# A decoder step on one core: second feed-forward weights in the other half's input buffers, closer decode gathers, spaced late loads

## The chip, the core and the metric

The kernel runs on one of the eight cores of a Trainium2 chip. A core has TensorE (PE, matrix products, with PEld its weight load), VectorE (DVE), ScalarE (ACT), GpSimd (POOL) and SyncE (SP, which here only issues transfers). Each engine executes its own instructions in order; semaphores order them against each other. The metric is the device time of one execution in microseconds (us), as the median of several runs.

## What is computed

One step of one hybrid decoder layer, for a prompt of 1024 tokens and for 8 samples with one new token each, whose past of 8192 tokens lies in a paged cache. All data are float32. The reference, cut to what matters:

```python
h = modulate(x, sh1, sc1)                        # layer norm, then shift and scale from c
sb_q, sb_k, sb_v, g_q, g_k, g_v, g_r, g_low, br_a, br_b = split(h @ w_in)
o_sb = sb_attend(sb_q, concat(past_k, sb_k), concat(past_v, sb_v), sb_bias)   # stick-breaking attention
o_g  = gla_mix(g_q, g_k, g_v, log_a, S0)         # gated linear attention, then norm and gate
merged = sigmoid(br_a) * (o_sb @ w_up_a) + sigmoid(br_b) * (o_g @ w_up_b)
x1 = layer_norm(ALPHA * x + gt1 * (merged @ w_o))
h2 = modulate(x1, sh2, sc2)
f  = square(relu(h2 @ w_ff1)) @ w_ff2            # 1024 -> 4096 -> 1024
x2 = layer_norm(ALPHA * x1 + gt2 * f)
```

It runs for the prompt (without a past) and for the samples (with the pages of the past, 268 MB of keys and values).

## The kernel before

**Precision.** A matmul of the prompt is made of three in the type float32r: each operand is split by `split` into a high part (`h`, copied by ACT) and a low part (`l`, the difference, by POOL or DVE), and high x high, low x high and high x low are added up in PSUM (`three`). So each weight tile is loaded raw by SP (`load_split`), split by ACT and POOL, and only then used by PE.

**Emission by an account.** The program is written out in one order by `Flow`: generators for the main stream (`main`), for two other streams and for many small tasks yield times or conditions; `Engines` keeps an account of when each engine and each tile would be ready, and the next piece of work is emitted where the account says it fits. `until(tiles)` waits for tiles to be ready by the account, `calm(t)` waits until DVE's backlog is at most `t` us by it. The account decides nothing on the chip, only the order of the instructions on each engine.

**Stages.** The 1024 prompt tokens are handled in two halves, n = 0 and 1, of 512 tokens. After the input projections, attention and linear attention come, for each half, `mix_in` (reloads the two branches' outputs), `mix_up` (up-projections, gates), `mix_out` (output projection in four quarters `cc`, residual, layer norm in its `finish`, which stores x1 to DRAM), in the order mix_up(0), mix_out(0), mix_up(1), mix_out(1). `second_in(n)` reloads x1, normalises it on DVE (`x`), transposes it on PE (`pT`), scales it on DVE (`h`) and splits it into the 16 tiles `h2h` and `h2l`: the inputs of the feed-forward part. Half 0 keeps them in the buffers `b1`, half 1 in `b2` (16 tiles of 2 KB per partition each); the same buffers held earlier inputs before. `ffn(0)` and `ffn(1)` come last.

**The feed-forward part.** The 4096 hidden columns are 32 units `u` of 128. A step is either `up(u)` (24 matmuls into `pmm`, then ACT `rl`, DVE `rl`, ACT `hidh`, DVE `hidl`) or a down step for a group of two units (8 output tiles, `pz` and `ptr` in turn, of 6 matmuls each, which DVE adds into `f`). The steps run up, up, down, with the down step one group behind. Each step's weights are loaded and split one step ahead: `wf` (first weights, called `wfh`/`wfl` after the split) and `wf2` (second weights, `wf2h`/`wf2l`; the trace calls their raw tile `wf` too). High parts come from a ring of 3 tiles (`N_W`), raw tiles and low parts from a ring of 6 (`N_RAW`), shared by both weights.

**The samples' decode.** It runs beside all this. For each of 8 samples 16 pieces of keys and 16 of values are gathered by POOL through an index (1 MB each, `kt` and `vt`, a ring of 3 tiles). A key piece is multiplied with the query on DVE (`kt`) and summed on DVE (`z`), two long operations that wait for `calm(K_CALM)`; a value piece takes 16 short matmuls into `va`. `K_PACE` gives the least distance between two gathers by the account, by stage: its fourth and fifth entries hold in ffn(0) and ffn(1). When decode has ended, `mix_sample` brings the samples to the feed-forward part; the units of ffn(1) that were already passed are loaded once more for the samples (`smp_late`: `wfs`, matmuls `pfs`), the later ones use ffn(1)'s own raw tiles.

## Time and profile before

| | |
|---|---|
| time, three runs | 2130.34, 2146.23, 2153.72 us; median 2146.23 us |
| the profiled execution | 2151.07 us, span of the trace 2149.4 us |
| PE busy | 1964.0 us (91%), granted clock 0.961 on average |
| DVE, POOL, ACT busy | 1483.2, 907.9, 710.0 us |
| read from memory | 475.93 MB, 236 GB/s over the span with what is written |

How to read it: PE is busy for most of the span. [...] Idle time of an engine is put down to what released it. Nearly all calls go through one helper, so rows are told apart by the names of the tiles, not by lines.

### The profile page before, as it was taken

To read this page: it belongs to the slowest core of one execution; us is meant where nothing else is said; L and a number is where in the kernel's file an instruction comes from. 1 tells how busy PE (TensorE), PEld (TensorE's weight loads), DVE (VectorE), ACT (ScalarE), POOL (GpSimd) and SP (SyncE) were. 2 spreads that over 40 slices of the span, in tenths; PEclk is the share of its full clock that TensorE was granted. 3 is DMA by queue.
4 is the path that set the end of the run, shared out by engine and by line. 5 is a ranking of instruction groups with operands and counts; after the bars stand their busy time and mean duration, and the time that the engine had idled before them with its cause. 6 is when DMAs were issued, how large, how long until landed. Compare 5 with 4: busy or idle time off the path is not lost. (4 is left out here: it accounts for less than half of the span.)

```text
span 2149.4 us, 28929 instructions
## 1 busy us (share of the span) xinstructions
PE 1964.0 (91%) x11300; PEld 1375.9 (64%) x11300; DVE 1483.2 (69%) x1778; ACT 710.0 (33%) x1154; POOL 907.9 (42%) x615
## 2 busy tenths in 40 slices
PE   5899998999999899998988899999989999899896
PEld 2676665566556666677776666677666666565574
DVE  6678787888768588667898879786788333522248
ACT  2324444454444543222322322222214322121122
POOL 2342233344333223265656446555455444232235
PEclk9999999999999799999998999999999999999998
DMA  7895677787666458989887777888676565456623
GB/s 247 266 330 197 200 265 255 261 268 264 226 219 231 143 197 280 332 297 327 292 287 254 247 242 248 293 290 284 230 262 211 188 228 198 148 160 183 208 88 118
DMA packets 281922, 508.55 MB, mean 237 GB/s; under 512 B 16325, under 2 KB 209189, under 8 KB 245946
## 3 DMA queue, kind: packets, MB, share of 16 engines
q0 software_dynamic: 36864, 268.45, 34.8%
q1 hardware_dynamic: 217378, 209.66, 31.0%
q10 hardware_dynamic: 27544, 28.59, 3.8%
q8 instruction: 89, 1.46, 0.3%
q14 instruction: 47, 0.39, 0.1%
HBM read 475.93 MB, written 30.71 MB: 236 GB/s over the span
## 5 line engine op out<-in xcount | busy, mean ns | idle before, releaser
L212 DVE TENSOR_TENSOR kt<-kt,qb 128x2048 f32<-128x2048 f32 x128 | 291.5, 2279 | 43.0 <-DMA kt<-in_cache_k,idx 42.4
L212 DVE TENSOR_REDUCE z<-kt 128x32 f32<-128x2048 f32 x128 | 291.8, 2281 | 1.7
L212 POOL TENSOR_TENSOR wfl<-wf,wfh 128x1024 fp32r<-128x1024 f32 x64 | 154.9, 2420 | 248.4 <-ACT wfh L212 184.0
L212 POOL DMA_INDIRECT kt<-in_cache_k,idx x128 | 133.1, 1040 | 255.5 <-PE va L336 85.0
L212 POOL DMA_INDIRECT vt<-in_cache_v,idx x128 | 133.8, 1046 | 246.4 <-PE va L336 122.7
L212 POOL TENSOR_TENSOR wf2l<-wf,wf2h 128x1024 fp32r<-128x1024 f32 x62 | 153.0, 2470 | 104.7 <-ACT wf2h L212 57.2
L336 PE MATMUL va<-vt,wT 128*8 128x512 f32 x1024 | 145.9, 630 | 13.6 <-DMA vt<-in_cache_v,idx 13.4
L212 ACT ACTIVATE wfh<-wf 128x1024 fp32r<-128x1024 f32 x64 | 67.4, 1054 | 245.2 <-PE ptr L336 185.2
L336 PE MATMUL pmm<-h2h,wfh 128*128 128x512 f32 x512 | 141.0, 409 | 2.5 <-ACT wfh L212 2.5
L336 PE MATMUL pmm<-h2l,wfh 128*128 128x512 f32 x512 | 136.4, 400 | 0.0
L336 PE MATMUL pmm<-h2h,wfl 128*128 128x512 f32 x512 | 133.3, 396 | 0.0
L212 DVE TENSOR_TENSOR f<-f,pz 128x512 f32<-128x512 f32 x104 | 71.2, 684 | 79.1 <-PE pz L336 78.4
L336 PEld LDWEIGHTS pmm<-h2h,wfh 128*128 128x128 f32 x512 | 94.9, 192 | 43.4 <-issue 13.7
L212 DVE TENSOR_TENSOR rl<-rl,pmm 128x512 f32<-128x512 f32 x64 | 43.7, 682 | 110.0 <-ACT rl L212 109.8
L336 PEld LDWEIGHTS pmm<-h2l,wfh 128*128 128x128 f32 x512 | 95.1, 189 | 33.3 <-issue 12.8
L336 PEld LDWEIGHTS pmm<-h2h,wfl 128*128 128x128 f32 x512 | 94.7, 188 | 27.1 <-issue 6.8
L212 DVE TENSOR_TENSOR f<-f,ptr 128x512 f32<-128x512 f32 x104 | 71.0, 684 | 57.4 <-PE ptr L336 57.0
L336 PE MATMUL pz<-wf2h,hidh 128*128 128x512 f32 x248 | 88.8, 425 | 23.7 <-ACT wf2h L212 20.4
L212 DVE TENSOR_TENSOR_SCAN kp<-kp,zcol 128x512 f32<-128x512 f32 (+3 forms) x96 | 97.9, 1032 | 4.2 <-ACT kp L212 3.4
L336 PE MATMUL pz<-wf2l,hidh 128*128 128x512 f32 x248 | 86.7, 418 | 12.5 <-POOL wf2l L212 12.5
L212 ACT ACTIVATE rl<-pmm 128x512 f32<-128x512 f32 x64 | 38.1, 595 | 153.7 <-PE pmm L336 144.6
L336 PE MATMUL ptr<-wf2h,hidh 128*128 128x512 f32 x248 | 84.4, 413 | 0.9 <-DVE f L212 0.8
(401 smaller groups left out, 4267.8 us busy)
## 6 DMA issues: line engine op xcount, KB each, us to landing
wf<-in_w_ff SPq DMA_DIRECT2D x128, 512.0 KB
ra<-in_w_ada SPq DMA_DIRECT2D x24, 1024.0 KB
wfs<-in_w_ff SPq DMA_DIRECT2D x40, 512.0 KB
wbr<-in_w_in SPq DMA_DIRECT2D x16, 512.0 KB
d_br<-brg ACTq DMA_DIRECT2D x32, 256.0 KB
g<-d_br SPq DMA_DIRECT2D x32, 256.0 KB
wo<-in_w_o SPq DMA_DIRECT2D x16, 512.0 KB
xt<-in_x_prompt SPq DMA_DIRECT2D x8, 512.0 KB
```

What stands on the lines that cost most here:

```text
L212: ins = f(*a, **k)
L336: ins = E.matmul(out, lhsT, rhs, start=start, stop=stop, **kw)
```

## The change

The buffers `b1` and `b2` become rings of 8 pairs (high and low part in one tile, with the same bytes). While half 1 has no input yet, ffn(0) keeps the split second weights of its groups up to u = 25 in `b2`; ffn(1) keeps those of all its groups in `b1`, which half 0 has left. Their loads are emitted two steps ahead (`ahead_`, `early`). `second_in(1)` is therefore emitted near the end of ffn(0). `mix_out` calls `after` in its first quarter, not its second. Some adds of the layer norms move from POOL to DVE. The pace of the decode gathers in the feed-forward part is shorter and the allowed backlogs are larger. `smp_late` puts 10 us between its loads.

```diff
-K_PACE, K_CALM = (12.0, 11.5, 14.0, 11.0, 10.0), 2.5
-A_PACE, SG_MAX, CALM = 7.0, 6, 1.0
+K_PACE, K_CALM = (12.0, 11.5, 14.0, 9.0, 8.0), 3.5
+A_PACE, SG_MAX, CALM = 7.0, 6, 2.5
...
-N_FA, N_DK = 8, 4
+N_FA, N_DK, N_LAST = 8, 4, 6
...
+    def pair(tag, name):
+        t = sb.tile([P, 2, 512], F32R, tag=tag, name=name, bufs=8)
+        return t[:, 0, :], t[:, 1, :]
     def b1(name):
-        return sb.tile([P, 512], F32R, tag="b1", name=name, bufs=16)
+        return pair("b1", name)
...
@@ sub_ln
-            (G, V)[h].tensor_tensor(xs[h][:n], xs[h][:n], b_t[h][:n], ALU.add)
+            V.tensor_tensor(xs[h][:n], xs[h][:n], b_t[h][:n], ALU.add)
@@ mix_out
-            if cc == 1 and after is not None:
+            if cc == 0:
                 after()
@@ second_in
             for kk in range(4):
                 k = 4 * hf + kk
+                yield 0.7
                 yield until(*xs, tr=True)
@@ smp_late
+                yield 10.0
                 go = []
                 flow.spawn(smp_up(rs, go))
-                yield lambda: bool(go)
                 rs = [raw([P, 2, 512], "wfs2") for y in range(2)]
...
-                yield until(*rs, *go)
+                yield 10.0
+                yield lambda: bool(go) and until(*rs, *go)()
@@ load_down
+                if x < 2 and (n or us[0] < NU - N_LAST):
+                    dst = tuple(
+                        sb.tile([P, 2, 512], F32R, tag=("b2", "b1")[n], name=nm, bufs=8) for nm in ("wf2h", "wf2l")
+                    )
@@ ffn
+        ahead_ = [ws]
+        def early(y):
+            us = steps[y][1] if y < len(steps) else None
+            return us is not None and len(us) == 2 and (n == 1 or us[0] < NU - N_LAST)
         for y, (x, us) in enumerate(steps[:-1]):
...
-            nxt = yield from load(*steps[y + 1])
+            while len(ahead_) < min(len(steps), y + (3 if early(y + 2) else 2)):
+                ahead_.append((yield from load(*steps[len(ahead_)])))
+            ws = ahead_[y]
+            if n == 0 and y == len(steps) - 3 * N_LAST // 2 + 1:
+                flow.spawn(second_in(1, h2b, b2))
...
-                    G.tensor_tensor(f[t][h], f[t][h], b_t[h], ALU.add)
+                    (V if n == 0 else G).tensor_tensor(f[t][h], f[t][h], b_t[h], ALU.add)
@@ main
-        flow.spawn(second_in(1, h2b, b2), 60.0)
```

What this does to the order is shown at three places. On ACT, in the middle of ffn(0), for two groups (`wfh` and `wf2h` are the high parts of first and second weights, `rl` and `hidh` belong to the up step whose `pmm` they read). Before:

```order
L212 ACTIVATE wfh_11503<-wf_11501 128x1024
L212 ACTIVATE wf2h_11547<-wf2_11545 128x1024
L212 ACTIVATE rl_11538<-pmm_11507 128x512
L212 ACTIVATE hidh_11541<-rl_11538 128x512
L212 ACTIVATE wf2h_11553<-wf2_11551 128x1024
L212 ACTIVATE rl_11586<-pmm_11557 128x512
L212 ACTIVATE hidh_11589<-rl_11586 128x512
```

and in the changed kernel:

```order
L212 ACTIVATE wfh_11290<-wf_11288 128x1024
L212 ACTIVATE rl_11157<-pmm_11128 128x512
L212 ACTIVATE hidh_11160<-rl_11157 128x512
L212 ACTIVATE wf2h_11294<-wf2_11296 128x1024
L212 ACTIVATE rl_11192<-pmm_11166 128x512
L212 ACTIVATE wf2h_11300<-wf2_11302 128x1024
L212 ACTIVATE wfh_11399<-wf_11397 128x1024
```

In PE's order the last matmul into `pmm_11507` stands 27 instructions ahead of the first use of `wf2h_11553`; the last one into `pmm_11128` stands 125 ahead of the first use of `wf2h_11294` (a down step and two up steps more).

On PE, at the end of mix_out(1) (`pbig<-woh`, `pbig<-wol`) and the head of ffn(0) (`pmm`), where `second_in(0)` transposes (`pT`). Before, its first transposes follow the last matmul of the output projection:

```order
L336 MATMUL va<-vt,wT 8x512 x4
L336 MATMUL pbig<-woh,ml 128x256 x4
L336 MATMUL pbig<-wol,mh 128x256 x8
L362 MATMUL pT_9967<-ident,x_9877 128x128
L362 MATMUL pT_9967<-ident,x_9880 128x128
L362 MATMUL pT_9967<-ident,x_9883 128x128
L362 MATMUL pT_9967<-ident,x_9886 128x128
L362 MATMUL pT_9978<-ident,x_9877 128x128
```

Now its first transposes stand between matmuls of the third quarter:

```order
L341 MATMUL pbig<-wol,mhl 128x256 x8
L367 MATMUL pT_9702<-ident,x_9600 128x128
L367 MATMUL pT_9702<-ident,x_9603 128x128
L367 MATMUL pT_9702<-ident,x_9606 128x128
L367 MATMUL pT_9702<-ident,x_9609 128x128
L341 MATMUL pbig<-woh,mhl 128x256 x12
L367 MATMUL pT_9726<-ident,x_9600 128x128
```

Six of the eight groups of four transposes have moved ahead of the end of the output projection, two still follow it.

On POOL, in the middle of ffn(0): gathers of keys and values (`kt`, `vt`) between the low parts of the weights. Before:

```order
L212 DMA vt_11522<-in_cache_v,idx_448 128x2048
L212 DMA kt_11530<-in_cache_k,idx_448 128x2048
L212 TENSOR_TENSOR wf2l_11548<-wf2_11545,wf2h_11547 128x1024
L212 DMA vt_11608<-in_cache_v,idx_448 128x2048
L212 DMA kt_11618<-in_cache_k,idx_448 128x2048
L212 TENSOR_TENSOR wf2l_11554<-wf2_11551,wf2h_11553 128x1024
L212 TENSOR_TENSOR wfl_11596<-wf_11593,wfh_11595 128x1024
L212 DMA vt_11674<-in_cache_v,idx_448 128x2048
L212 TENSOR_TENSOR wfl_11679<-wf_11676,wfh_11678 128x1024
```

and in the changed kernel:

```order
L212 TENSOR_TENSOR wfl_11291<-wf_11288,wfh_11290 128x1024
L212 DMA vt_11164<-in_cache_v,idx_432 128x2048
L212 TENSOR_TENSOR wf2l_11295<-wf2_11296,wf2h_11294 128x1024
L212 DMA kt_11217<-in_cache_k,idx_432 128x2048
L212 DMA kt_11228<-in_cache_k,idx_432 128x2048
L212 DMA vt_11242<-in_cache_v,idx_432 128x2048
L212 TENSOR_TENSOR wf2l_11301<-wf2_11302,wf2h_11300 128x1024
L212 TENSOR_TENSOR wfl_11400<-wf_11397,wfh_11399 128x1024
L212 DMA vt_11278<-in_cache_v,idx_432 128x2048
```

There are now up to three gathers in a row between two splits. Over ffn(0) the key products in DVE's order come to 5, 5, 5, 5, 5, 4, 3 for each two groups from the second pair on before, and to 5, 6, 6, 6, 7, 7, 0 now; the last `va` stands 240 feed-forward matmuls (of 3024) earlier.

## Rows read from the trace of the kernel before

**Rows 1.** Busy time of each engine by stretch (end of mix_up(1) with mix_out(1), head of ffn(0), rest of ffn(0), first part of ffn(1), rest of ffn(1), end). Columns: window and its length in us, then busy us and instructions of PE, PEld, DVE, ACT, POOL, the granted clock, the share of the DMA engines' time, GB/s.

```profile
1030.00:1150.00 120.00, 105.61 (x652) 86.75 (x650) 109.97 (x140) 28.50 (x40) 75.22 (x47) 0.96 0.86 292
1150.00:1194.00 44.00, 36.94 (x151) 25.59 (x152) 39.69 (x45) 14.65 (x23) 27.75 (x21) 0.81 0.72 245
1194.00:1609.00 415.00, 390.63 (x1743) 275.80 (x1742) 330.88 (x327) 113.99 (x151) 226.34 (x137) 0.96 0.77 265
1609.00:1840.00 231.00, 221.62 (x1042) 151.91 (x1041) 104.01 (x143) 68.43 (x93) 109.36 (x63) 0.97 0.62 202
1840.00:2128.00 288.00, 261.15 (x1576) 173.60 (x1575) 113.11 (x203) 65.18 (x97) 84.62 (x37) 0.96 0.50 154
2128.00:2149.40 21.40, 5.65 (x25) 4.32 (x23) 17.08 (x22) 3.90 (x7) 15.56 (x11) 0.70 0.25 98
```

**Rows 2.** Waits of PE from 1150 to 2128 us: which tile it wrote, the engine and tile that it waited for, then us in total, times, longest us.

```profile
PE pz L336 <- ACT wf2h L212: 20.4, 11, 5.7
PE pz L336 <- POOL wf2l L212: 12.5, 7, 6.0
...
PE pT L362 <- DVE x L212: 5.5, 4, 3.8
PE pT L362 <- DVE h L212: 3.9, 2, 3.2
PE pfs L336 <- DMA wfs<-in_w_ff: 3.7, 4, 2.0
...
PE pfs L336 <- DVE hs L212: 2.2, 3, 1.5
...
PE ptr L336 <- DVE f L212: 0.8, 1, 0.8
```

**Rows 3.** The timeline of all engines around one wait for `wf2h`: start us, us, engine, line, operation, output and inputs, in brackets the idle time before it and what ended it.

```profile
1524.62 2.40 POOL L212 TENSOR_TENSOR wf2l<-wf,wf2h 128x1024 fp32r<-128x1024 f32 x1
1524.66 2.92 DVE L212 TENSOR_TENSOR hidl<-rl,hidh 128x512 fp32r<-128x512 f32 x1 [0.70 <-ACT hidh L212]
...
1527.50 2.27 DVE L212 TENSOR_TENSOR kt<-kt,qb 128x2048 f32<-128x2048 f32 x1
...
1530.41 0.63 ACT L212 ACTIVATE hidh<-rl 128x512 fp32r<-128x512 f32 x1 [2.16 <-DVE rl L212]
...
1532.04 0.51 PE L336 MATMUL pz<-wf2h,hidh 128*128 128x512 f32 x1 [3.49 <-ACT wf2h L212]
```

**Rows 4.** A stretch of ffn(0) in which PE does not wait: all engines as in rows 1, then the same stretch for the operations on `kt` alone (DVE busy, POOL busy, clock, DMA share, GB/s).

```profile
1400.00:1500.00 100.00, 100.00 (x462) 72.08 (x460) 79.06 (x73) 28.25 (x36) 55.65 (x35) 1.00 0.82 286
...
1400.00:1500.00 100.00, 42.20 (x19) 8.82 (x9) 1.00 0.82 286
```

**Rows 5.** From the timeline of PE: waits for the second weights in the last groups of ffn(0).

```profile
1591.12 0.79 PE L336 MATMUL pz<-wf2l,hidh 128*128 128x512 f32 x1 [6.02 <-POOL wf2l L212]
...
1608.24 0.50 PE L336 MATMUL pz<-wf2l,hidh 128*128 128x512 f32 x1 [1.03 <-POOL wf2l L212]
```

**Rows 6.** Windows around four of the waits for `wf2h` and `wf2l`, columns as in rows 1.

```profile
1530.00:1550.00 20.00, 17.96 (x77) 12.63 (x78) 12.71 (x13) 4.54 (x5) 10.26 (x6) 0.91 0.62 216
1680.00:1710.00 30.00, 26.38 (x111) 18.53 (x110) 10.80 (x17) 8.75 (x12) 13.78 (x7) 0.89 0.51 170
1860.00:1890.00 30.00, 22.79 (x91) 17.42 (x91) 15.45 (x23) 8.17 (x12) 13.74 (x6) 0.83 0.21 59
1920.00:1950.00 30.00, 26.42 (x156) 16.20 (x155) 7.93 (x16) 5.08 (x7) 7.16 (x3) 0.89 0.49 143
```

**Rows 7.** From the timeline of PE: transposes of `second_in(0)` at the head of ffn(0).

```profile
1150.95 1.12 PE L362 MATMUL pT<-ident,x 128*128 128x128 f32 x4 [3.25 <-DVE h L212]
...
1158.61 0.80 PE L362 MATMUL pT<-ident,x 128*128 128x128 f32 x4 [0.73 <-DVE x L212]
1163.21 1.14 PE L362 MATMUL pT<-ident,x 128*128 128x128 f32 x4 [3.81 <-DVE x L212]
```

**Rows 8.** Groups of equal operations: the adds of `xr` on POOL (950 to 1170 us) and on DVE (1030 to 1170), `x` and `h` of `second_in(1)` on DVE (1194 to 2090), with busy us, mean ns and idle before; then for two tiles shortest, median and longest ns of one.

```profile
L212 POOL TENSOR_TENSOR xr<-xr,row 128x512 f32<-128x512 f32 x5 | 7.4, 1485 | 14.3 <-DVE xr L212 14.3
...
L212 DVE TENSOR_TENSOR xr<-xr,row 128x512 f32<-128x512 f32 x12 | 16.4, 1388 | 1.8 <-ACT xr L212 1.6
...
L212 DVE TENSOR_SCALAR x<-x,x_mu 128x512 f32<-128x512 f32 x8 | 8.6, 1111 | 0.6 <-DMA x<-d_x 0.6
...
L212 DVE TENSOR_SCALAR h<-pT,adaT 128x512 f32<-128x512 f32 x8 | 6.2, 800 | 0.4 <-PE pT L362 0.4
...
L212 DVE TENSOR_TENSOR xr<-xr,row x24: 676/693/3922, 1024.7 to 1220.5; 128x512 f32<-128x512 f32 x24
...
L212 DVE TENSOR_TENSOR hidl<-rl,hidh x64: 667/692/3003, 1176.1 to 2112.7; 128x512 fp32r<-128x512 f32 x64
```

**Rows 9.** The two DVE operations of a key piece, 1194 to 2090 us: busy us, mean ns, idle before.

```profile
L212 DVE TENSOR_TENSOR kt<-kt,qb 128x2048 f32<-128x2048 f32 x36 | 82.1, 2280 | 4.5 <-DMA kt<-in_cache_k,idx 4.5
L212 DVE TENSOR_REDUCE z<-kt 128x32 f32<-128x2048 f32 x36 | 82.0, 2279 | 0.2
```

**Rows 10.** The gathers on POOL, 1194 to 2090 us: busy us, mean ns, idle before them and what ended it.

```profile
L212 POOL DMA_INDIRECT vt<-in_cache_v,idx x58 | 57.3, 988 | 89.7 <-PE va L336 62.9 <-DVE z L212 14.4 <-PE ptr L336 4.5
L212 POOL DMA_INDIRECT kt<-in_cache_k,idx x34 | 33.5, 986 | 43.4 <-DVE z L212 24.2 <-PE va L336 16.4 <-issue 1.1
```

**Rows 11.** The matmuls of the decode's value pieces over the whole span: shortest, median and longest ns of one, first and last start.

```profile
L336 PE MATMUL va<-vt,wT x1024: 592/596/1061, 248.0 to 1818.4; 128*8 128x512 f32 x171
```

More of the change, by code (lines that the diff above doesn't have):

```diff
@@ L559, in ada @@
         yield 0.0
-    hhi = [[(b1, b2)[n](f"hhi{k}_{n}") for n in range(2)] for k in range(8)]
-    hlo = [[(b1, b2)[n](f"hlo{k}_{n}") for n in range(2)] for k in range(8)]
+    hhl = [[(b1, b2)[n](f"hhl{k}_{n}") for n in range(2)] for k in range(8)]
+    hhi = [[x[0] for x in y] for y in hhl]
+    hlo = [[x[1] for x in y] for y in hhl]
     hsT = cp.tile([P, 8, 32], F32, name="hsT")
@@ L1780, in ffn @@
                 flow.spawn(residual())
-            ws = nxt
-        us = groups[-1]
+        us, ws = groups[-1], ahead_[-1]
         nxt = ahead and ahead()
```

8 lines of the change are left out of this document (4 added, 4 removed).

## The prediction

> **What bounds the kernel now.** I read first the busy time by stretch [rows 1]. TensorE (PE) is the bound: the part that the change is about runs from 1150 us, where the first sums of the feed-forward half 0 begin, to 2128 us, and there PE works 36.9 + 390.6 + 221.6 + 261.2 = 910 of 978 us. It executes the same matmuls before and after (the order holds 9222 PE instructions in both), so time can come only from two places: from PE's idle time, 978 - 910 = 68 us here, and from the work that it does at the lower granted clock. [...] The last 21.4 us of the span [rows 1] are the end of the last layer norm, which the change leaves as it is.
>
> Then I read who kept PE waiting there [rows 2]. Two lines stand out: `wf2h` on ScalarE (ACT) 20.4 us and `wf2l` on GpSimd (POOL) 12.5 us, the high and low part of the second feed-forward weights. One such wait in full is in [rows 3]: PE gets `wf2h` at 1532.04 after 3.49 us of idling. The weights are not late from memory; ACT is in order, and the `wf2h` split stands behind `hidh`, which waits 2.16 us for DVE's `rl`, which stands behind a 2.27 us product of the decode (`kt`). So a chain of three in-order engines sits between the split and its place, because in the old order the split is issued one up-projection ahead of its use.
>
> **The change part by part.** I make the sum against the profiled execution (span 2149.4 us, its own time 2151.07 us, 4.8 us above the median of the three runs).
>
> *Second weights two steps ahead.* The order rows of ACT show it: before, `wf2h_11553` follows `hidh_11541`, whose up-projection ends 27 PE instructions ahead of the first use of that weight; now `wf2h_11294` follows the work of an up-projection that ends 125 PE instructions ahead of it. At the mean of one PE instruction in the quiet stretch (462 in 100 us, [rows 4]) that is 6 us against 27 us, and the longest wait for these tiles was 6.0 us [rows 2]. So where the new buffers are used the waits should go entirely. They are not used for the last three groups of half 0 (u from 26 up); there stand waits of 6.02 and 1.03 us [rows 5], 7 us, which I leave in. Removed: 20.4 + 12.5 - 7 = 25.9 us. I take 24, with 12 and 26 as bounds (12: half of the waits come back somewhere else in the in-order queues).
>
> *The clock behind these waits.* After each the granted clock is down for a while. In the windows around them [rows 6] busy time times (1 - clock) is 17.96 x 0.09 + 26.38 x 0.11 + 22.79 x 0.17 + 26.42 x 0.11 = 11.3 us, and smaller dips lie elsewhere. It goes where the wait goes, though not each dip need have that wait alone as its reason. I take 11, bounds 5 and 14.
>
> *The second layer norm's input earlier.* `after` now runs at the first quarter of the output projection, and `second_in(0)` is emitted there. The PE rows show what moves: six of the eight groups of four transposes now stand between the output projection's matmuls, where before all eight stood behind its last matmul, in a clump at the head of the feed-forward part. In that stretch, 1150 to 1194, PE idles 44 - 36.9 = 7.1 us, and at clock 0.81 its busy time loses 7.0 us more [rows 1]; the waits are those for DVE's `x` and `h` [rows 7]. 14 us at most. I take 11, bounds 0 and 14: DVE, which makes `x` and `h`, is busy 110 of the 120 us ahead of it [rows 1], so some of the wait may reappear there. `second_in(1)` moves from the first third of half 0 to its end, behind the last group that uses the second half's buffers; its waits before were at most 1 us (the `x` line of [rows 2] less the 0.73 and 3.81 us of [rows 7]), so I cost it at nothing. Its cover is the last groups' 22 us each of matmuls; without it, it would cost the same clump again, 14 us.
>
> *Samples' late loads.* Decode ends about 240 feed-forward matmuls of 3024 earlier, so 14 units instead of 20 are loaded a second time (12 DMAs of 512 KB less on SP's queue), and with 10 us between them. The waits of PE that belong to it are 3.7 + 2.2 = 5.9 us for `pfs` [rows 2] and a clock dip. I take 4, bounds 0 and 8.
>
> *Adds from POOL to DVE.* 8 adds of `xr` and 8 of `f` (128x512) move. On POOL an `xr` add took 1.49 us, on DVE 1.39 on average (0.69 when nothing disturbed it) [rows 8]. The 8 for `xr` add 8 x 1.39 = 11 us to a DVE that is busy 110 of 120 us from 1030 to 1150 (half of them fall there). PE can come to wait for DVE there, so the cost lies between 0 and 11 us; I take 2, since the finish steps wait for a calm DVE and `x1` is now needed no sooner than before. The 8 for `f` fall at the start of half 1, where DVE is busy 104 of 231 us: nothing.
>
> *Gathers closer together.* Pace 11 to 9 and 10 to 8. In the DVE order half 0 has 5 `kt` products for two groups before and 6 to 7 after. Each costs two operations of 2.28 us [rows 9]. In the quiet stretch DVE is busy 79.06 of 100 us, 42.2 of it decode [rows 4]; two groups take about 48 us there, so 7 instead of 5 make it 79 + 2 x 4.56 x 100/48 = 98 of 100. That just fits, while the work of `second_in(1)` comes on top at the end (eight `x` and eight `h`, 8.6 + 6.2 us in [rows 8]). Decode has the same total, so later stretches get it back, but PE is held only by what is late at once. Bounds 0 and 25; I take 7. DMA: at 286 GB/s its share is 0.82 in that stretch [rows 4]; two more gathers of 1 MB in 48 us are 44 GB/s, which makes it 0.95. That is a transfer system near its full share too, but the second weights now have 27 us of lead.
>
> *Pairs in one tile.* The hi and lo halves share a tile; the matmuls on the hi half still wait for ACT alone in the order, so it costs nothing. Everything ahead of 1030 us is only reordered by the changed account; nothing there says which way: 0, bounds -10 and +10.
>
> **Sum.** -24 - 11 - 11 - 4 + 2 + 7 = -41: 2151 - 41 = 2110, and against the median of before 2146 - 41 = 2105. I forecast **2107 us**, between the two.
>
> **The rivals.**
> 1. *DVE becomes the bound of half 0.* The 98 of 100 above leaves no room, and `hidl` took 2.92 us beside a `wf2l` on POOL [rows 3] where its median is 0.69 us [rows 8]. If the accumulations into `f` come late behind 2.28 us products, PE waits on them. Price: over the dense last six groups, 140 us, the excess of `second_in(1)` (14.8 us) plus as much again in clock dips: 25 to 30 us given back, so 2130 to 2135. Against it: dots are only emitted while DVE's backlog is below 3.5 us, and PE waited only 0.8 us for `f` on DVE in the whole part [rows 2]. Chance 0.16. [...]
> 2. *The waits stay where they are.* If the wait is made by the order of ACT (behind `hidh`) and not by the lead, the first two terms fall away and only 11 + 4 - 9 = 6 us remain: 2140. Against it the 125 instructions in the order. Chance 0.06.
> 3. *Slower: POOL's queue.* A gather waits on POOL for a free buffer, and the splits stand behind it. POOL idled 62.9 us for `va` and 14.4 + 24.2 us for `z` ahead of gathers [rows 10]. Now two gathers stand in a row ahead of a split, and `wfl`, the first weights' low part, still has a lead of one step. Up to now PE never waited for `wfl`. If it did in each of the some 25 groups that run beside the decode, with 2 us and as much again of clock: 100 us lost, 2151 - 41 + 100 = 2210; the change is a loss once 11 of these groups are hit. For it: the closer gathers wait more often. Against: half a group's time of slack on POOL (55.6 of 100 us busy, [rows 4]). Chance 0.09.
>
> **How the numbers follow.** Forecast case 0.69 with its own range: all gains at their upper bounds, 26 + 14 + 14 + 8 = 62, no cost, and 10 from the reordered head give 2146 - 72 = 2074; all at the middle of the lower half, about 25 net, give 2121. Rivals 1 and 2 end at 2130 to 2140. Range for 8 in 10: **2074 to 2140**; outside are rival 3 (0.09) and the far ends. Two runs of this kernel differ by up to 1%, so 1% (21 us) is what can be told from no change: faster by more than 1% (below 2125) is the forecast case, 0.69; within 1% rivals 1 and 2, 0.22; slower 0.09.
>
> **What would show it.** Right: in the changed profile PE's waits for `wf2h` and `wf2l` sum to about 7 us, all at the end of half 0; no clump of `pT` waits at the head of the feed-forward part; clock above 0.97 from 1194 on; the last `va` (at 1818 us before [rows 11]) comes some 80 us earlier. Wrong: PE waiting for `f` on DVE (rival 1), for `wfl` or `wfh` (rival 3), or for `pT`/`tmp` inside the output projection (the adds); or the head before 1030 us longer by more than 10 us.

## The result, and the profile after

| | before | changed |
|---|---|---|
| median | 2145.74 us (17 runs) | 2131.93 us (17 runs, 2118.06 to 2144.01) |
| ratio, 95% interval | | 0.9945 [0.9919, 0.9971] |
| profiled execution, span | 2151.07, 2149.4 us | 2141.47, 2139.7 us |

The changed kernel is 14 us faster, where 39 were forecast (2146 to 2107 us). That is inside the range, and less than the 1% that the prediction gave as just told from no change. Its profiled execution is 9.5 us above its median, which has to be kept in mind below. One execution each of ring3_cut and lead_half1_pace below was slow, and their medians leave it out.

Windows of the changed kernel, as in [rows 1] by stage: end of mix_up(1) with mix_out(1), head of ffn(0), rest of ffn(0), first part of ffn(1) up to the last `va`, rest of ffn(1), end.

```profile
1042.20:1161.40 119.20, 109.16 (x674) 89.43 (x673) 102.12 (x145) 37.78 (x50) 70.31 (x42) 0.97 0.82 276
1161.40:1192.20 30.80, 26.27 (x123) 18.80 (x123) 26.49 (x32) 12.87 (x20) 24.44 (x15) 1.00 0.73 242
1192.20:1658.90 466.70, 422.06 (x1865) 293.76 (x1864) 386.01 (x369) 122.32 (x160) 229.85 (x147) 0.94 0.75 265
1658.90:1787.40 128.50, 124.49 (x593) 81.75 (x589) 60.29 (x85) 43.22 (x61) 69.03 (x39) 0.99 0.74 259
1787.40:2122.00 334.60, 329.87 (x1960) 237.99 (x1960) 148.18 (x257) 86.08 (x124) 106.11 (x46) 0.99 0.44 134
```

I read the first two numbers and the clock together: a stretch loses its length less PE's busy time, and, by an estimate that the prediction used too, the busy time times one minus the clock. The clock is the share of full speed that the profile gives TensorE. In the changed kernel it was 0.50 from 1203.39 to 1207.66 us, and there a down step's matmuls (128x512) started every 0.43 us (10 in 4.27 us); from 1650.02 to 1657.38 us it was 1.00, and they started every 0.23 us (32 in 7.36 us). The head of ffn(0) loses 4.5 + 0 us, where before it lost 14 [rows 1]. Half 1 (the last two rows) loses 4.0 + 1.2 + 4.7 + 3.3 = 13 us, where before its rows give 53. But the rest of ffn(0) loses 44.6 + 0.06 x 422.06 = 70 us, where 1194 to 1609 gave 40. So two places gained 10 and 40 us, and the third took 30 of these 50 back.

Where in half 0 that loss lies, in the changed kernel (first three rows) and in the kernel before (last two):

```profile
1192.00:1292.00 100.00, 78.51 (x310) 56.51 (x309) 78.39 (x80) 30.98 (x44) 45.66 (x26) 0.85 0.61 208
1392.00:1492.00 100.00, 87.15 (x366) 59.97 (x365) 76.77 (x62) 23.27 (x29) 51.37 (x33) 0.89 0.75 264
1592.00:1658.90 66.90, 64.43 (x307) 41.94 (x306) 64.36 (x76) 18.42 (x24) 36.60 (x23) 1.00 0.78 279
1191.00:1291.00 100.00, 90.19 (x382) 60.59 (x382) 77.53 (x90) 34.08 (x50) 47.68 (x30) 0.93 0.73 250
1391.00:1491.00 100.00, 100.00 (x465) 71.20 (x464) 78.85 (x73) 28.69 (x36) 56.16 (x36) 1.00 0.83 291
```

The two stretches of 100 us lose 33 and 22 us, where before they lost 16 and nothing, with VectorE (DVE) busy 78 and 77% of them. In the last stretch, where DVE is busy 96%, PE loses 2.5 us.

PE's waits in half 0 (1192 to 1659 us), as in [rows 2]:

```profile
PE va L341 <- DMA vt<-in_cache_v,idx: 29.2, 14, 6.9
PE pz L341 <- ACT f L212: 5.0, 1, 5.0
...
PE ptr L341 <- DVE f L212: 2.9, 1, 2.9
PE pz L341 <- DVE hidl L212: 2.6, 1, 2.6
PE pz L341 <- POOL wf2l L212: 1.2, 1, 1.2
```

The waits for `wf2h` are gone and those for `wf2l` are 1.2 us, from 20.4 and 12.5 [rows 2]. In their place PE waits for the decode's value pieces. Over the whole span:

```profile
PE va L341 <- DMA vt<-in_cache_v,idx: 53.8, 27, 6.9
```

and over the whole span before:

```profile
PE va L336 <- DMA vt<-in_cache_v,idx: 13.4, 10, 2.5
```

Three more views answer to rows of before. The gathers on POOL from 1192 to 2090 us [rows 10] wait longer for a buffer that a value product frees (`PE va`), 90.2 us in place of 62.9; the last `va` starts at 1786.8 us in place of 1818.4 [rows 11], 32 us earlier and not 80; and the output projection's first matmul of mix_out(0) starts at 976.0 us, where before it started at 965.5, so the head is 10 us longer.

```profile
L212 POOL DMA_INDIRECT vt<-in_cache_v,idx x61 | 63.2, 1037 | 120.8 <-PE va L341 90.2 <-DVE z L212 22.6 <-issue 3.1
```

```profile
L341 PE MATMUL va<-vt,wT x1024: 592/596/1061, 265.2 to 1786.8; 128*8 128x512 f32 x171
```

```profile
L341 PE MATMUL pbig<-woh,mhl x512: 274/282/583, 976.0 to 1159.2; 128*128 128x256 f32 x171
```

and the last of these before:

```profile
L336 PE MATMUL pbig<-woh,mh x256: 274/281/583, 965.5 to 1143.5; 128*128 128x256 f32 x128
```

### The profile page after: what moved, and what is told of

It reads as the page before. It is cut to its first block, busy times and chain, and to the rows that moved or that the text cites. A ratio compares the mean times of both kernels' runs of the same rounds, so it can differ in the third digit from the quotient of the medians.

```text
span 2139.7 us, 28864 instructions
## 1 busy us (share of the span) xinstructions
PE 1965.1 (92%) x11300; PEld 1390.5 (65%) x11300; DVE 1492.7 (70%) x1796; ACT 716.6 (33%) x1158; POOL 877.2 (41%) x597
## 3 DMA queue, kind: packets, MB, share of 16 engines
q8 instruction: 89, 1.46, 0.3%
## 5 line engine op out<-in xcount | busy, mean ns | idle before, releaser
L341 PE MATMUL pmm<-h,wfh 128*128 128x512 f32 x1024 | 270.3, 407 | 1.8 <-ACT h L212 1.0
L341 PEld LDWEIGHTS pmm<-h,wfh 128*128 128x128 f32 x1024 | 190.9, 192 | 81.1 <-issue 35.6
L341 PE MATMUL va<-vt,wT 128*8 128x512 f32 x1024 | 142.6, 618 | 53.9 <-DMA vt<-in_cache_v,idx 53.8
L341 PE MATMUL pmm<-hhl,wbrh 128*128 128x512 f32 x512 | 144.3, 414 | 1.8 <-ACT brg L212 1.8
L341 PE MATMUL pmm<-h,wfl 128*128 128x512 f32 x512 | 133.8, 398 | 0.0
L341 PEld LDWEIGHTS pmm<-hhl,wbrh 128*128 128x128 f32 x512 | 91.6, 190 | 37.3 <-issue 18.1
L341 PEld LDWEIGHTS pmm<-h,wfl 128*128 128x128 f32 x512 | 95.2, 189 | 31.6 <-issue 11.2
L341 PE MATMUL pz<-wf2h,hidh 128*128 128x512 f32 x248 | 83.7, 416 | 7.4 <-ACT f L212 6.9
L341 PE MATMUL pz<-wf2h,hidl 128*128 128x512 f32 x248 | 82.4, 410 | 2.6 <-DVE hidl L212 2.6
```

The costliest lines, as they stand in the source:

```text
L341: ins = E.matmul(out, lhsT, rhs, start=start, stop=stop, **kw)
```

## The experiments

Each time is a median beside runs of the kernel before on the same chip; the ratio is to these. "Half 0" is ffn(0) from its first down step on, "half 1" is ffn(1) up to the last down step, and "loss" is reckoned from windows as above. The clock has two digits there, which alone leaves some 2 us open, and each loss is read from one execution. Two executions of one order differ by 12 us (spacing_back below), so only larger differences are read. The profile of pace_back is 14 us above its median, that of buffers_only 14 us below.

### Parts undone

**The pace, `pace_back`.**

```diff
-K_PACE, K_CALM = (12.0, 11.5, 14.0, 9.0, 8.0), 3.5
+K_PACE, K_CALM = (12.0, 11.5, 14.0, 11.0, 10.0), 3.5
```

> The changed kernel with the old pace of the gathers in the feed-forward part (11 and 10 by the account, not 9 and 8). Theory A (the value gathers are late because the account prices their landing too short, and PE, no longer held up by the splits, now reaches their matmuls at the time the account meant): PE still waits for vt 35 to 50 us in all, and the time is within 0.4% of the changed kernel. Theory B (the closer gathers crowd the transfers): the waits of PE for vt fall to the 13 us of before, and the time to about 2110 us. Theory C (the larger allowed DVE backlog frees the gather buffers late): as A, no change.

2166.85 us, ratio 1.010 [1.006, 1.014]. Half 0 keeps 27.6 us of waits for value pieces, so the pace alone does not make them, and it loses 57.8 + 0.06 x 412.2 = 83 us, more than in the changed kernel. What the kernel is slower by lies at the end, from the last down step (2124.6 us) on. Half 0 and the end:

```profile
1193.00:1663.00 470.00, 412.20 (x1797) 290.25 (x1796) 353.12 (x351) 117.86 (x155) 215.45 (x135) 0.94 0.68 238
2124.60:2178.80 54.20, 27.47 (x237) 12.14 (x235) 17.37 (x40) 6.14 (x12) 6.27 (x5) 0.65 0.57 181
```

Decode ends at 1889 us, more units have to be loaded late, and with 10 us between the loads the samples become the end of the kernel: 54 us in place of 18. So the spacing needs the early end of decode that the closer pace brings.

**The backlogs, `calm_back`.**

```diff
-K_PACE, K_CALM = (12.0, 11.5, 14.0, 9.0, 8.0), 3.5
-A_PACE, SG_MAX, CALM = 7.0, 6, 2.5
+K_PACE, K_CALM = (12.0, 11.5, 14.0, 9.0, 8.0), 2.5
+A_PACE, SG_MAX, CALM = 7.0, 6, 1.0
```

> The changed kernel with the old allowed DVE backlogs (K_CALM 2.5, CALM 1.0). Theory C: PE's waits for vt fall to 15 to 25 us and the time to about 2115 us. Theories A and B: the waits for vt stay at 35 to 55 us, time within 0.5% of the changed kernel; decode ends some us later.

2133.42 us, 0.9951 [0.9915, 0.9988]: the same. But the time is made up otherwise. Half 0 (1215.5 to 1641 us) waits 7.8 us for value pieces and 12.8 us for `f` on DVE, and loses 29 + 8 = 37 us, with the closer pace and the longer lead both in place and DVE busy 86%:

```profile
1215.50:1641.00 425.50, 396.45 (x1796) 283.76 (x1793) 367.83 (x345) 114.97 (x151) 222.10 (x137) 0.98 0.76 263
```

On the other side the first matmul of mix_out(0) comes at 991.6 us, 16 us later than in the changed kernel. The transposes of `second_in(0)` come at 1167.2 us, behind the last matmul of the output projection, although `after` runs in the first quarter, and the head of ffn(0) loses 19 us (1163.8 to 1215.5), where the changed kernel loses 5 and the kernel before 15. So the larger backlogs won time ahead of half 0; in the sum of the prediction they have no term.

**The buffers alone, `buffers_only`**: pairs, second weights two steps ahead, `second_in(1)` late; all else as before.

```diff
-K_PACE, K_CALM = (12.0, 11.5, 14.0, 9.0, 8.0), 3.5
+K_PACE, K_CALM = (12.0, 11.5, 14.0, 11.0, 10.0), 2.5
-A_PACE, SG_MAX, CALM = 7.0, 6, 2.5
+A_PACE, SG_MAX, CALM = 7.0, 6, 1.0
...
-            if cc == 0:
+            if cc == 1 and after is not None:
                 after()
```

(and the adds, the 0.7 in `second_in` and the late loads as before).

> Of the change only the pairs of buffers, the second weights two steps ahead and with them the late second input; old pace, old backlogs, adds on POOL, the hook in the second quarter, late loads as before. Theory A: the waits for wf2h and wf2l are gone (33 us to under 5 outside the last groups), but those for vt rise from 13 to 30 us or more, so most of the gain is lost: 2125 to 2145 us. Theory B and C: the waits for vt stay at 13 us and the time falls by 25 to 35 us, to 2110 to 2120 us.

2165.69 us, 1.0116 [1.007, 1.0163]: slower than the kernel before. The first matmul of mix_out(0) comes at 984.5 us, 19 us later than before, and ahead of it nothing but the pairs and the order that the account makes with them differs. The orders of PE up to there are the same in this kernel and in calm_back (984.5 and 991.6 us). How the pairs cost that time is not settled. In the whole span PE waits 45.9 us for value pieces and 22 us for `f` on DVE. Half 0 (1201 to 1650.5 us) loses 56 us, more than before (41), and half 1 loses 22, less than before (51).

**The late loads, `spacing_back`.**

```diff
-                yield 10.0
                 go = []
                 flow.spawn(smp_up(rs, go))
+                yield lambda: bool(go)
...
-                yield 10.0
-                yield lambda: bool(go) and until(*rs, *go)()
+                yield until(*rs, *go)
```

> The changed kernel with the old late loads of the samples, without the 10 us between them; nothing is left out. The prediction's term for them is 4 us (0 to 8). Theory: decode ends early enough in the changed kernel that the samples are not the end (their last sums at 2097 us, PE's last at 2122), so the spacing brings only the 3.7 us of waits that PE had for raw weights: 2132 to 2140 us. Rival (the spacing costs, since it delays the samples): 2125 us or less.

2128.01 us, 0.9926 [0.9889, 0.9963], against 0.9945 [0.9919, 0.9971]: with the closer pace the spacing is worth nothing that can be measured. Up to the end of half 0 this kernel stands in the same order as the changed one, and its profile has 453 us there (loss 58) in place of 467 (70). So two executions of one order can differ by 12 us in this stretch, and its loss in the changed kernel is best taken as 58 to 70. The reckoning itself is loose too: the same work up to mix_out(0) in the same 976 us comes out as a loss of 107 us in the changed kernel and 118 in half_low.

### The waits for value pieces

**A longer landing in the account, `land_late`.**

```diff
+G_LATE = 2.5
...
-                est.moved(out, out, est.place(self.name, max(t, est.flow.t), 1.04))
+                est.moved(out, out, est.place(self.name, max(t, est.flow.t), 1.04), G_LATE)
```

(`moved` adds the last argument to the time at which the tile is there.)

> The changed kernel, but the account prices the landing of each gather 2.5 us later, so that the products are emitted that much later behind their gathers; nothing else. Theory A: PE's waits for vt fall from 53.8 us to under 15, the clock in half 0 of the feed-forward part rises to 0.97 or more, and the time falls by 30 to 50 us, to 2080 to 2100 us. Theory B: the products are later too, so the waits fall in part (to 25 to 35 us), but the gathers that are crowded still land late; 2110 to 2125 us. Theory C: in between, as buffers are held 2.5 us longer, which costs decode time; no gain in the total.

2196.18 us, 1.0255 [1.0207, 1.0304]. All three theories miss. The waits fall from 53.8 to 37.0 us, in half 0 only from 29.2 to 25.1, and half 0 loses 88 us. Decode ends at 1931 us, so that the spaced samples take 79 us behind the last down step.

**No wait at all, `no_value_wait` and `before_no_value_wait`.**

```diff
                     va[32 * r : 32 * r + 8], wT[:, r, j, :], vt[:, 512 * r : 512 * r + 512],
-                    start=j == 0, stop=j == 15,
+                    start=j == 0, stop=j == 15, stand=ones[:, None, :].to_broadcast([P, 4, P]),
```

(`mm` gives the matmul `stand` in place of its last operand and charges the account as before.)

> The changed kernel, in which the matmuls of a decode value piece read a constant tile of ones in place of the gathered piece: the gathers, the account and all other work stay, only the use of the gathered values is left out (the samples' attention is not that of the reference). PE then cannot wait for a gather of values, and the gather's buffer is free as soon as it has landed. Theory A (the gain that is missing went into PE's waits for value pieces, 53.8 us in the changed kernel, and the clock behind them; in the feed-forward half 0 idle time and half of the low-clock time rose by 33 us): 2060 to 2085 us. Rival B (the closer gathers crowd the transfers, the waits for value pieces only show it first): the waits come back at the splits of the weights or at raw weights, 2110 us or more.

> The kernel before with the same replacement: value matmuls read ones, the use of the gathered values is left out. Its waits for value pieces were 13.4 us. Theory A: 2122 to 2132 us, so that between this and the changed kernel with the same replacement lie 40 to 70 us, the size that the prediction summed. Rival B: between the two lie 20 us or less, about what the two whole kernels differ by.

2134.94 us, 0.995 [0.992, 0.9979], and 2159.76 us, 1.0088 [1.0051, 1.0125]. Theory A falls. All 53.8 us of waits are gone, and the time is that of the changed kernel. Nor did the waits move to the splits or the raw weights, as rival B had it: 3.1 us for `wf2h` are all of that kind in half 0. PE's waits in half 0 (1192 to 1649 us):

```profile
PE pz L341 <- DVE hidl L212: 9.9, 1, 9.9
PE pz L341 <- DVE f L212: 8.6, 6, 2.5
PE pz L341 <- ACT f L212: 6.4, 1, 6.4
PE pT L367 <- DVE x L212: 5.4, 2, 3.2
```

Idle time there is 44.5 us, as with the waits, and it is now mostly DVE that PE waits for. The two kernels differ by 25 us, between what theory A and rival B had, because the kernel before became 17 us slower.

**A ring of four, `ring3_cut` and `ring4_cut`.**

```diff
-N_HK, N_MID, N_RAW, N_W, N_KV = 9, 9, 6, 3, 3
+N_HK, N_MID, N_RAW, N_W, N_KV = 6, 8, 6, 3, 3
```

and, in ring4_cut alone,

```diff
-        return sb.tile(list(shape), F32, tag="kv", name=name, bufs=N_KV)
+        return sb.tile(list(shape), F32, tag="kv", name=name, bufs=N_KV + 1)
```

> The changed kernel with fewer working tiles (hk 6 instead of 9, mid 8 instead of 9), nothing else: the partner of the next run, since a fourth gather buffer finds room only so. Both theories: somewhat slower than the changed kernel, 2135 to 2165 us, with some 50 us of waits of PE for value pieces.

> As ring3_cut, but the ring of gather buffers has four tiles on the chip, while the account still reckons with three. Theory A2 (the ring of three makes a loop: a gather waits on POOL until PE has read the oldest piece, lands some 7 us later, and PE reaches it before that): POOL's waits for va go, PE's waits for value pieces fall under 20 us, 30 to 45 us faster than ring3_cut. Rival A1 (the gathers are issued too late by the account whatever the ring, since it prices their landing at some 5 us): the waits stay above 35 us and the two differ by less than 10 us. Rival B (transfers): the landing gets longer, no gain.

2185.28 us, 1.0202 [1.0129, 1.0274], and 2184.02 us, 1.0218 [1.0155, 1.0281]. Fewer working tiles cost more than was expected. The fourth buffer takes the waits for value pieces from 36.6 to 6.2 us, as A2 said, and nothing is gained: in half 0 of ring4_cut (1229 to 1698 us) PE waits elsewhere.

```profile
PE pz L341 <- ACT hidh L212: 11.5, 1, 11.5
PE pz L341 <- DVE f L212: 10.4, 4, 7.1
PE ptr L341 <- DVE f L212: 8.7, 3, 5.1
PE va L341 <- DMA vt<-in_cache_v,idx: 5.2, 2, 3.5
```

### VectorE, and GpSimd beside it

**A light sum, `light_sum` and `before_light_sum`.**

```diff
-        V.tensor_reduce(z[:, :, :, j], kt.rearrange("p (r h d) -> p r h d", r=4, h=8), AX.X, ALU.add)
+        k4 = kt.rearrange("p (r h d) -> p r h d", r=4, h=8)
+        V.tensor_reduce(
+            z[:, :, :, j], k4, AX.X, ALU.add, real=(z[:, :, :, j], k4[:, :, :, 0:8], AX.X, ALU.add)
+        )
```

(the chip gets `real`, the account is charged for the whole.)

> The changed kernel, in which the sum over a key piece (z, 2.28 us on VectorE) reads only 8 of the 64 columns of each head, so that it takes some 0.4 us; the account still charges the whole. What is left out: 7/8 of each key product's sum. Theory D (behind the value pieces VectorE is the next that PE waits for in the feed-forward half 0, so that neither limit alone gives anything when it is taken away): the waits for value pieces stay, 2110 to 2130 us, a gain of under 20 us. Theory E (VectorE alone is the bound of half 0; the value pieces are late because z frees their buffers late): 2070 to 2100 us. Rival B (transfers): no gain.

> The kernel before with the light sum alone (z reads 8 of 64 columns of each head; 7/8 of each key product's sum left out), the partner of light_sum (2066 us). Theory E (VectorE, fuller in half 0 by the closer key pieces, takes back what the change gains): its own waits for wf2h and wf2l stay and only the part ahead of the feed-forward gets shorter, 2100 to 2120 us, so that the change is worth 35 to 55 us once VectorE is light, the size that the prediction summed. Rival (a lighter VectorE helps both kernels alike, and the change is small whatever VectorE does): 2070 to 2085 us, the two differ by 15 us or less.

2066.11 us, 0.9635 [0.9617, 0.9654], and 2099.26 us, 0.9775 [0.9715, 0.9835]. With a light VectorE the change is worth 33 us, with the full one 14. By the profiles some 10 of these 19 us lie ahead of mix_out(0): with the light sum both kernels reach it at the same time (937.9 and 937.7 us), with the full one the changed kernel comes 10 us later. By ratios it is 0.9635 / 0.9775 = 0.986 against 0.9945; the intervals leave the first open by some 0.006, so the two can only just be told apart. The place shows more. Half 0 of the changed kernel, then of the kernel before, both with the light sum:

```profile
1152.00:1576.00 424.00, 401.57 (x1858) 283.96 (x1856) 298.65 (x363) 119.63 (x157) 231.68 (x147) 0.98 0.81 286
```

```profile
1162.00:1580.00 418.00, 396.43 (x1790) 284.51 (x1789) 284.30 (x330) 111.89 (x147) 222.79 (x137) 0.98 0.77 264
```

Losses of 30 and 30 us, where with the full sum they are 58 to 70 and 41. DVE is busy 70% of the stretch here, 83% in the changed kernel. The waits for value pieces in half 0 fall too, from 29.2 to 13.9 us, though gathers and account are the same: they fall with VectorE's work. The transfers carry 286 GB/s at a share of 0.81, more than in the changed kernel (265), so they were not what held it (rival B). The time is what theory E had.

**Both off, `light_sum_no_value_wait` and `before_light_sum_no_value_wait`** (the two edits together).

> As light_sum, and the value matmuls read ones as in no_value_wait, so that both limits are off; the sum and the use of the values are left out as said there. Theory D: idle time in half 0 falls from 44 us to under 20, 2060 to 2095 us. Rival B: 2110 us or more, with the waits at the splits or raw weights.

> The kernel before with both limits off in the same way. Theory D: its own waits (for wf2h and wf2l) stay, 2115 to 2145 us, so that the changed kernel with both limits off is faster than this by 35 to 60 us: the size that the prediction summed is there, once neither the value pieces nor VectorE take it back. Rival B: the two differ by 25 us or less.

2106.94 us, 0.9826 [0.9808, 0.9844], and 2149.47 us, 1.0035 [1.0013, 1.0057]. The change is worth 43 us here. But taking the value waits from light_sum costs 41 us, which no theory said, and half 0 loses 58 us again although `z` is light. One wait of half 0 of the first kernel, from the timelines of POOL and DVE:

```profile
1345.80 0.95 POOL L213 DMA_INDIRECT kt<-in_cache_k,idx  x1 [6.08 <-DMA wf<-in_w_ff]
1346.76 4.74 POOL L213 TENSOR_TENSOR wf2l<-wf,wf2h 128x1024 fp32r<-128x1024 f32 x2
1351.44 2.35 POOL L213 TENSOR_TENSOR wfl<-wf,wfh 128x1024 fp32r<-128x1024 f32 x1
```

```profile
1347.61 6.74 DVE L213 TENSOR_TENSOR hidl<-rl,hidh 128x512 fp32r<-128x512 f32 x1
1354.27 0.68 DVE L213 TENSOR_TENSOR f<-f,pz 128x512 f32<-128x512 f32 x1
```

`hidl`, 0.69 us at the median in this half 0, takes 6.74: it ends 0.6 us behind the third split in a row on POOL, and the additions into `f` stand behind it. PE waited 4.62 us for that `f`. `hidl` in half 0 by kernel, the kernel before (1191 to 1618 us):

```profile
L212 DVE TENSOR_TENSOR hidl<-rl,hidh 128x512 fp32r<-128x512 f32 x31 | 32.2, 1038 | 9.0 <-ACT hidh L212 9.0
```

the changed kernel (1192 to 1659),

```profile
L212 DVE TENSOR_TENSOR hidl<-rl,hidh 128x512 fp32r<-128x512 f32 x31 | 41.0, 1323 | 7.4 <-DMA d_x<-xr 3.8 <-PE ptr L341 1.8 <-ACT hidh L212 1.3
```

and light_sum_no_value_wait (1158 to 1610):

```profile
L213 DVE TENSOR_TENSOR hidl<-rl,hidh 128x512 fp32r<-128x512 f32 x31 | 49.9, 1609 | 21.8 <-ACT hidh L213 18.8 <-DMA d_x<-xr 2.0 <-PE ptr L342 0.7
L213 DVE TENSOR_TENSOR kt<-kt,qb 128x2048 f32<-128x2048 f32 x40 | 91.1, 2277 | 1.5 <-DMA kt<-in_cache_k,idx 1.5
L213 DVE TENSOR_TENSOR f<-f,pz 128x512 f32<-128x512 f32 x52 | 35.4, 680 | 8.8 <-PE pz L342 8.3
```

As I read the timeline, the second weights two steps ahead bring two `wf2l` and a `wfl` together on POOL, and that no gather has to wait for PE any more packs them closer still; no run separates the two.

**Shorter splits, `half_low`.**

```diff
-        split(r, h, lo)
+            S.activation(h, r, AF.Copy)
+            hf = h.bitcast(F32)
+            G.tensor_tensor(lo, r, hf, ALU.subtract, real=(lo[:, 0, :], r[:, 0, :], hf[:, 0, :], ALU.subtract))
...
-(ws[x][0][:, cc, :], ws[x][1][:, cc, :]))
+(ws[x][0][:, cc, :], ws[x][1][:, 0, :]))
```

> The changed kernel, in which only half of each wf2l is made on GpSimd (1.2 us in place of 2.4) and read for both halves; the other half of the low part of the second weights is left out. Theory F (the splits of weights that now stand in a row on GpSimd stretch VectorE's hidl, 19.6 us over 31 of them in half 0 against 10.8 before, and the additions into f behind it): hidl's stretch falls under 12 us and the time to 2105 to 2120 us. Theory E without F: under 8 us of gain.

2107.42 us, 0.9818 [0.9762, 0.9875]: 25 us faster than the changed kernel, in the range of theory F. Half 0 (1189 to 1630 us) and `hidl` in it:

```profile
1189.00:1630.00 441.00, 409.75 (x1867) 285.66 (x1865) 369.35 (x369) 121.94 (x159) 195.15 (x147) 0.98 0.79 279
```

```profile
L213 DVE TENSOR_TENSOR hidl<-rl,hidh 128x512 fp32r<-128x512 f32 x31 | 32.9, 1062 | 10.9 <-DMA d_x<-xr 7.2 <-ACT hidh L213 3.3 <-PE ptr L342 0.3
```

The loss is 31 + 8 = 39 us in place of 58 to 70, though the waits for value pieces (23.4 us) stay. The edit also frees POOL itself for 35 us of the stretch; that the stretched DVE operation is the way, and not POOL's queue, is argued from the timelines. Two other kernels speak against `hidl` alone, calm_back (1215.5 to 1641 us) and lead_half1 (below, 1184 to 1666 us):

```profile
L212 DVE TENSOR_TENSOR hidl<-rl,hidh 128x512 fp32r<-128x512 f32 x30 | 47.4, 1580 | 7.5 <-ACT hidh L212 4.6 <-DMA d_x<-xr 2.7
L212 DVE TENSOR_TENSOR hidl<-rl,hidh 128x512 fp32r<-128x512 f32 x31 | 29.1, 938 | 13.9 <-ACT hidh L212 9.6 <-DMA d_x<-xr 4.3
```

The first stretches it more than the changed kernel and loses 37 us in half 0, the second hardly at all and loses 86.

**Less work on VectorE, `square_on_act`.**

```diff
-            V.tensor_tensor(rl, rl, p, ALU.mult)
+            S.activation(rl, rl, AF.Square)
```

> The changed kernel, in which the square of the hidden columns is made by ScalarE (a third ACT operation on rl) and not by VectorE (0.69 us, 32 times in each half). Nothing is left out. Theory E: 21 us of VectorE's work less in half 0, and hidh no longer waits behind key products: by the ratio of light_sum (some 44 us of loss in half 0 for 75 us of work) 10 to 15 us, 2110 to 2125 us. Rival (VectorE is not the bound): 2130 us or more.

2145.46 us, 0.9995 [0.9963, 1.0027]: slower than the changed kernel by 13 us, against theory E. DVE's busy time in half 0 falls to 365 us of 479, and the loss is 75 us all the same; 23.9 us of it are waits for value pieces and 5.6 us for `wfh` on ACT. So it is not DVE's busy share as such. Of the edits that leave work out, those that shorten the long operations which the short ones stand behind (`z` from 2.28 to 0.41 us, the splits from 2.4 to 1.3) brought the loss of half 0 down; moving short operations to ACT did not.

### Other versions

**`calm_by_stage`.**

```diff
-K_PACE, K_CALM = (12.0, 11.5, 14.0, 9.0, 8.0), 3.5
+K_PACE, K_CALM = (12.0, 11.5, 14.0, 9.0, 8.0), (3.5, 3.5, 3.5, 2.5, 2.5)
...
-                yield calm(CALM)
+                yield calm(1.0)
...
-                yield 10.0
+                yield 3.0
```

(1.0 in the layer norm of ffn alone, 3.0 at both places of `smp_late`.)

> The changed kernel with the old allowed backlogs in the feed-forward part alone (2.5 us for key products from there on, 1.0 us for its layer norm; the new ones stay ahead of it), and 3 us instead of 10 between the samples' late loads. Nothing is left out. Theory D: key products then stand less in the way of the additions into f, the idle time of half 0 falls from 44.6 us to some 30 and decode ends some 20 us later without the samples becoming the end: 2100 to 2120 us. Otherwise: 2125 us or more.

2175.14 us, 1.0123 [1.0096, 1.015]. Decode ends at 1900 us instead of 1787, and both halves lose: half 0 still 71 us, half 1 42. In half 0 it has the backlogs of calm_back, which lost 37 there: with the same rules there, what comes before must matter, and which part of it is not known.

**`lead_half1`, `lead_half1_pace`** (both with the late loads of spacing_back).

```diff
-                if x < 2 and (n or us[0] < NU - N_LAST):
+                if x < 2 and n:
...
-            return us is not None and len(us) == 2 and (n == 1 or us[0] < NU - N_LAST)
+            return us is not None and len(us) == 2 and n == 1
```

and in the second also

```diff
-K_PACE, K_CALM = (12.0, 11.5, 14.0, 9.0, 8.0), 3.5
+K_PACE, K_CALM = (12.0, 11.5, 14.0, 11.0, 7.0), 3.5
```

with `second_in(1)` spawned from `main` as before.

> spacing_back (2128 us), in which the second weights stand two steps ahead in half 1 alone; in half 0 they are loaded and split one step ahead as before. Nothing is left out. Theory E with F (in half 0 VectorE and GpSimd's splits in a row take back what the longer lead brings, in half 1, where VectorE is less than half busy, the lead brings its whole gain): half 0 is no slower without the lead, 2110 to 2130 us. Rival (the lead is worth its waits in half 0 as well): the waits for wf2h and wf2l come back there, some 15 us and clock behind them, 2140 to 2155 us.

> As lead_half1, with the old pace of the gathers in half 0 (11) and a closer one in half 1 (7 in place of 8), and the input of half 1 made early in half 0 as before. Nothing is left out. 31 value pieces fall into half 0 in place of 43. Theory E: VectorE is lighter in half 0, its loss falls to about that of before (41 us) while half 1 stays at some 12 to 15: 2100 to 2120 us, faster than both kernels. Rival (decode then ends too late, or its pieces are late in half 1): 2130 us or more.

2141.1 us, 0.9997 [0.9967, 1.0027], and 2143.33 us, 0.9993 [0.996, 1.0025]. Without the lead in half 0 the kernel is 13 us slower than spacing_back: the rival holds, at the closer pace the lead is worth its waits there too. And a slower pace in half 0 with a closer one in half 1 only moves the loss. No version tried here without leaving work out beats the changed kernel by more than can be measured. The losses together, from windows of each profile, with DVE's busy share and the mean length of `hidl` in half 0:

| kernel | half 0, us | half 1, us | DVE busy, half 0 | `hidl`, half 0, us |
|---|---|---|---|---|
| before | 41 | 51 | 80% | 1.04 |
| changed | 70 | 13 | 83% | 1.32 |
| spacing_back | 58 | 14 | 84% | 1.23 |
| pace_back | 83 | 21 | 75% | 1.46 |
| calm_back | 37 | 15 | 86% | 1.58 |
| buffers_only | 56 | 22 | 78% | 1.62 |
| calm_by_stage | 71 | 42 | 80% | 1.19 |
| lead_half1 | 86 | 6 | 78% | 0.94 |
| lead_half1_pace | 37 | 55 | 80% | 1.08 |
| square_on_act | 75 | 11 | 76% | 1.30 |
| no_value_wait | 57 | 27 | 85% | 1.43 |
| before_light_sum | 30 | 41 | 68% | 1.23 |
| light_sum | 30 | 16 | 70% | 0.94 |
| light_sum_no_value_wait | 58 | 33 | 70% | 1.61 |
| half_low | 39 | 6 | 84% | 1.06 |

Neither of the last two columns orders the losses of half 0.

## Why the prediction was wrong

**What bounds the kernel.** The premise holds: the traces hold 11300 matmuls of PE in both kernels (the prediction counted 9222). The terms for the clock price a loss at busy time times one minus the clock; that is an estimate of mine, and no run shows their size by itself. What is shown is the pace of the same matmuls at two clocks: 0.43 us each at 0.50, 0.23 us at 1.00.

**Second weights in half 1.** Right: the waits of half 1 for `wf2h` and `wf2l` (17.3 of the 32.9 us of [rows 2]) are gone, and half 1 lost 13 us in place of 51, more than the 31 that the terms for it came to (17.3 of waits, 9.7 of clock by [rows 6], 4 for the late loads). buffers_only, without the closer pace, has 22 there. The lead is not enough by itself, though: lead_half1_pace has it in half 1 and loses 55.

**The step that failed is the sum for half 0: "Second weights two steps ahead" with its clock, and "Gathers closer together" ("Bounds 0 and 25; I take 7"), each priced alone.** By the terms half 0 should have lost about 41 - 8.6 (15.6 of the 32.9 us of waits fall there, and 7 were left in) - 1.6 (clock, [rows 6]) + 7 = 38 us; it lost 58 to 70. "The waits should go entirely" came true: 15.6 us became 1.2, and the 7 us that were left in went as well. But time did not follow: PE now waited elsewhere, 29.2 us for value pieces, and the clock, forecast above 0.97 from 1194 us on, was 0.94 in half 0. The wrong size is not that of the gathers alone: with the old pace and the lead half 0 loses 83 us (pace_back), with the closer pace and no lead 86 (lead_half1), with neither 37 (lead_half1_pace, which has `second_in(1)` early, as before). So by these profiles the lead, which was to bring 10 us there and at worst half of its waits, brings nothing by itself in half 0 and is worth something only beside the closer pace. The larger backlogs have no term at all; with the old ones (calm_back) half 0 loses 37 us, what the terms came to, and the time is lost ahead of it.

**Why half 0 loses more is open.** Shown is what it is not: not the waits for value pieces (no_value_wait, ring4_cut), not the transfers (light_sum). A light `z` or half of the `wf2l` splits takes 19 to 40 us of the loss away, so the work of VectorE and GpSimd has a part in it. But calm_back comes as low with all the work in place, and light_sum_no_value_wait loses 58 with the light `z`. How the in-order queues interlock, which is what each edit changes, was not isolated.

**Rival 1.** Its price, 2130 to 2135 us, came true, its mechanism is not shown. The 98 of 100 us that I reckoned for DVE did not come: it was busy 83% of half 0, PE lost most where it was busy 77 to 78%, and almost nothing where it was busy 96%. Waits for `f` on DVE, the sign that I named, are 3.3 us in the changed kernel. The 0.8 us of such waits before, by which I gave it 0.16, told little, as I read it now: the splits held PE up first.

The 2.92 us `hidl` beside a 2.40 us `wf2l`, which rival 1 named [rows 3], came larger in light_sum_no_value_wait: 6.74 us beside three splits in a row. How the splits stretch it was not isolated.

**The second layer norm's input.** The time came: the two stretches from 1030 to 1194 lost 18.6 + 14.1 us [rows 1], and 13.3 + 4.5 after: 15 us, where I took 11. The reason is only half right. With the early `after` and the old backlogs (calm_back) the transposes still stand behind the output projection, and the head of ffn(0) loses 19 us; it took the larger backlogs as well.

**Pairs and the head.** Pairs were put at nothing, since the matmuls on the high half still wait for ACT alone, and the head at 0 with bounds of 10. With the pairs and no other part of the change ahead of it, mix_out(0) came 19 us later (buffers_only), with the larger backlogs as well 10 (the changed kernel). So this term was mis-sized too; the sign that I named, a head longer by more than 10 us, came just so (976.0 against 965.5).

**Late loads.** -4 us forecast, nothing measured. What they do was missed: with a later end of decode the spacing makes the samples the end (pace_back, land_late).

**Adds.** +2 us forecast; no edit undid them alone.

**The range.** That the time lies inside it is luck in part: half 1 gained more than was summed, half 0 and the head lost what was not.

**Rivals 2 and 3.** The split waits did not stay, and PE did not wait for `wfl`; both fall.

**What else stays open.** Why square_on_act loses, why before_no_value_wait is 17 us slower than the kernel before (its waits for `wf2l` rise from 12.5 to 24.7 us), and how much of half_low's gain is POOL's queue.

## What to carry to other kernels

When a wait of the bounding engine is to be removed, do not count it as time before asking what else comes due in the same in-order queues. Here the removed waits became time in the half where VectorE was less than half busy (45% of half 1 in the changed kernel), and other waits took their place in the half where gathers, splits and VectorE's work run dense. The name on a wait tells who was last, not who is the limit: take the wait away by other data and see whether the time moves before building on it. A part of a change that only shifts the order, like an allowed backlog or two tiles put into one, needs a term too. And test the parts in pairs, not only one by one: the lead and the closer pace each raised the loss of half 0 alone, and raised it less together.

## What the runs showed of the hardware

- A VectorE subtraction with both inputs in SBUF (`hidl`), 0.69 us at its median, took 6.74 us beside three GpSimd splits in a row, and 1.61 us on average over that half 0 (light_sum_no_value_wait). There `kt` and the additions of `pz` into `f`, each with one input in PSUM, kept their means of 2.28 and 0.68 us.
- Four profiles of one PE order up to mix_out(0) (the changed kernel, pace_back, calm_by_stage, half_low) reached it between 976.0 and 980.7 us. Two of them, the changed kernel and half_low, came at 976.0 and 976.1 us at granted clocks of 0.97 and 0.95. PE was busy for 895.9 and 903.4 us of it: the 7.5 us more at the lower clock came out of PE's idle time, and the head was not longer.
